# Fused RMSNorm and matmul: a new order of the first loads, of the first matmuls, of the norms, and single stores at the end

## The chip, the cores and the metric

The kernel runs on one core of a Trainium2 chip. The time is device microseconds of one execution, the median of several. A run's state is "fast" or "slow" (over 1.5% above the fastest of its kernel); verdicts use fast runs: the medians below are of all six times, the ratios of fast ones alone. Profiles come from one execution each. Their span is about 1.8 us shorter than the time of the same run.

## The reference

```python
def reference(x, gamma, weight, eps):      # x: 16 x 1024 x 512, weight: 512 x 768, float32
    rms = np.sqrt(np.mean(x ** 2, axis=-1, keepdims=True) + eps)
    x_norm = x / rms * gamma
    return np.matmul(x_norm, weight).astype(np.float32)
```

That is 16384 rows, in 128 tiles of 128 rows. 33.6 MB of x and 1.6 MB of weights come in and 50.3 MB go out.

## The kernel before

GpSimd casts x to bfloat16, TensorE transposes it (pairs of bfloat16 as one 32-bit word, so that a tile takes two transposes, called "words" below), VectorE copies the transpose out of PSUM, TensorE multiplies by the weights (gamma folded in) in four k steps, each one matmul of 512 columns and one of 256. ScalarE squares and sums rows, takes the root, VectorE the reciprocal. The result is scaled by it while it is evicted (copied out of PSUM), even tiles by ScalarE, odd ones by VectorE. Large loads and stores all go through one queue, that of the sync engine. Parts that the change and the argument touch (cuts marked; NT is the 128 tiles, NP the 64 pairs of them, K the 4 k steps; the lists say how many tiles one load of x or one store takes):

```python
    XG, OG = 16, 8
    AHEAD = 20
    ...
    opening = [1, 2, 1, 2, 2]
    last = NT // OG - 1
    x_first, x_size = stretches(XG, {0: opening + [4, 4], 1: [4, 4, 8]})
    o_first, o_size = stretches(OG, {0: opening, 1: [4, 4], last - 1: [4, 4], last: [2, 2, 2, 1, 1]})
    ...
    xin = ctx.enter_context(tc.tile_pool(name="xin", bufs=2))      # two groups of 16 tiles of x
    ...
        load_until(3)                                  # x tiles 0, then 1 and 2
        w_f32 = singles.tile([P, K, O], F32)
        for h in range(2):                             # the two weight halves
            nc.sync.dma_start(out=w_f32[:, 2 * h:2 * h + 2, :].rearrange("p c o -> p (c o)"), in_=wv[:, h, :])
        load_until(2 * XG)
    ...
        for k in (0, 1):
            for i in range(3):
                matmuls(i, acc[i], [k])
        root(0, 3, ssq)
        weights(2, nc.vector)
        weights(3, nc.scalar)
        cast(3, nc.gpsimd)
        matmuls(0, acc[0], [2, 3])
        finish_tile(0, acc[0], nc.scalar)
        transpose_tile(3)
        norms(3, 1)
        matmuls(1, acc[1], [2, 3])
        finish_tile(1, acc[1], nc.vector)
    ...
        for j in range(2, NP):                         # pairs of tiles
            load_until(2 * j + AHEAD)                  # from group 2 on: 16 tiles in one load
            if j + 3 < NP:
                cast(2 * j + 6, nc.gpsimd, 2)
            if j + 1 < NP:
                norms(2 * j + 2, 2)
            ...
            for i, engine in ((2 * j, nc.scalar), (2 * j + 1, nc.vector)):
                a = accumulator()
                matmuls(i, a, range(K), feed)          # feed: transposes of pair j + 2 in between
                finish_tile(i, a, engine)              # evict, and store when a stretch is full
```

Of the kernel before, what the change touches and what calls it, by code (L numbers as in the profile page):

```python
# [12 lines left out]
F32 = mybir.dt.float32  # L13
# [5 lines left out]
def kernel(  # L19
# [8 lines left out]
    nc = tc.nc  # L28
    P = 128

    x = x.flatten_outer_dims()
    out = out.flatten_outer_dims()
    N, D = x.shape
    _, O = out.shape
    K = D // P
    NT = N // P
    NP = NT // 2
    XG, OG = 16, 8
    AHEAD = 20
    WIDE = 512  # L40



# [2 lines left out]
    def stretches(group, parts):  # L46
        first, size, i = {}, {}, 0
        for g in range(NT // group):
            for n in parts.get(g, [group]):
                for t in range(i, i + n):  # L50
                    first[t], size[t] = i, n
                i += n
        return first, size

    opening = [1, 2, 1, 2, 2]
    last = NT // OG - 1
    x_first, x_size = stretches(XG, {0: opening + [4, 4], 1: [4, 4, 8]})
    o_first, o_size = stretches(OG, {0: opening, 1: [4, 4], last - 1: [4, 4], last: [2, 2, 2, 1, 1]})

    def rows(ap, i, n):  # L60
        if i < XG:
# [3 lines left out]
    singles = ctx.enter_context(tc.tile_pool(name="singles", bufs=1))  # L65
# [11 lines left out]
    def held(tiles, group, i, n=1):  # L77
        return tiles[i // group][:, i % group:i % group + n, :]

    def load(i):  # L80
        if i // XG not in x_tiles:
            x_tiles[i // XG] = xin.tile([P, XG, D], F32, name="xt")
        nc.sync.dma_start(out=held(x_tiles, XG, i, x_size[i]), in_=rows(x, i, x_size[i]))  # L83
# [3 lines left out]
    def load_until(i):  # L87
        while starts and starts[0] < i:
            load(starts.pop(0))

    def cast(i, engine, n=1):
        if i // 2 not in xb_tiles:
            xb_tiles[i // 2] = xbp.tile([P, 2, D], BF16, name="xb")
        engine.tensor_copy(out=xb_tiles[i // 2][:, i % 2:i % 2 + n, :], in_=held(x_tiles, XG, i, n))  # L94

    def square(i, ssq):
        jk = junk.tile([P, D], BF16, name="jk")
        nc.scalar.activation(out=jk, in_=held(x_tiles, XG, i)[:, 0, :], func=AF.Square, accum_out=ssq)  # L98

    def root(i, n, ssq):  # L100
        rms = stats.tile([P, 4], F32, name="rms")
        nc.scalar.activation(out=rms[:, :n], in_=ssq[:, :n], func=AF.Sqrt, scale=1.0 / D, bias=eps_sb)  # L102
        rstd = stats.tile([P, 4], F32, name="rstd")
        nc.vector.reciprocal(out=rstd[:, :n], in_=rms[:, :n])  # L104
        for t in range(n):
            rstd_of[i + t] = rstd[:, t:t + 1]

    def norms(i, n):
        ssq = stats.tile([P, 4], F32, name="ssq")
        for t in range(n):  # L110
            square(i + t, ssq[:, t:t + 1])
        root(i, n, ssq)
# [3 lines left out]
    def transpose_word(j, t, h):  # L116
        if j not in tp_tiles:
            tp_tiles[j] = tpsum.tile([P, 2, 2, P], F32, name="tp")
        words = xb_tiles[j].rearrange("p a d -> p (a d)").bitcast(F32)
        lo = t * (D // 2) + h * P  # L120
        nc.tensor.transpose(out=tp_tiles[j][:, t, h, :], in_=words[:, lo:lo + P], identity=ident_f)  # L121
# [9 lines left out]
    def transpose_tile(i):  # L131
        for h in range(2):
            transpose_word(i // 2, i % 2, h)
        evac(i // 2, i % 2, 1)
# [7 lines left out]
    def accumulator():  # L142
        return opsum.tile([P, 2, WIDE], F32, name="ops").rearrange("p a b -> p (a b)")

# [15 lines left out]
    def matmuls(i, acc, ks, feed=None):  # L160
        for k in ks:
            matmul(i, k, acc, 0, WIDE)
            if feed:
                feed()
            matmul(i, k, acc, WIDE, O)

    def finish_tile(i, acc, engine):
        scale(engine, out_tile(i), acc[:, :O], rstd_of[i])
        store(i)
# [14 lines left out]
        return feed  # L184

    with tc.manual_schedule():
        g_row = singles.tile([2, P, 2], F32)
        nc.scalar.dma_start(out=g_row, in_=gamma.rearrange("(h w c) -> h w c", w=P, c=2))

        wv = weight.rearrange("(h w c) o -> w h (c o)", w=P, c=2)  # L190
        touched = singles.tile([P, 2, 1], F32)
        nc.scalar.dma_start(out=touched, in_=wv[:, :, 0:1])
        nc.scalar.preload_act_table(AF.Sqrt)  # L193
        load_until(3)
        w_f32 = singles.tile([P, K, O], F32)
        for h in range(2):
            nc.sync.dma_start(out=w_f32[:, 2 * h:2 * h + 2, :].rearrange("p c o -> p (c o)"), in_=wv[:, h, :])
        load_until(2 * XG)


        warm = singles.tile([P, WIDE], BF16)
        nc.vector.memset(warm, 0.0)  # L202
        eps_sb = singles.tile([P, 1], F32)
        nc.vector.memset(eps_sb, float(eps))  # L204
        ident_f = singles.tile([P, P], F32)
        make_identity(nc, ident_f)
        spare = accumulator()

        def warm_up(n):
            for _ in range(n):  # L210
                nc.tensor.matmul(out=spare[:, :WIDE], lhsT=warm[:, :P], rhs=warm, start=True, stop=True)  # L211

        w_bf = singles.tile([P, K, O], BF16)

        def weights(k, engine, lo=0, hi=O):
            scale(engine, w_bf[:, k, lo:hi], w_f32[:, k, lo:hi], g_sb[:, k % 2, k // 2:k // 2 + 1])


        ssq = stats.tile([P, 4], F32, name="ssq")
        warm_up(6)  # L220
        cast(0, nc.vector)
        square(0, ssq[:, 0:1])
        gp = tpsum.tile([P, 2, 2], F32, name="tp")
        for c in range(2):
            nc.tensor.transpose(out=gp[:, c, :], in_=g_row[:, :, c], identity=ident_f[:2, :2])  # L225
        g_sb = singles.tile([P, 2, 2], F32)
        nc.vector.tensor_copy(out=g_sb, in_=gp)  # L227
        transpose_tile(0)
        warm_up(3)
        cast(1, nc.vector)  # L230
        cast(2, nc.gpsimd)
        square(1, ssq[:, 1:2])
        square(2, ssq[:, 2:3])
        transpose_tile(1)
        transpose_tile(2)
        warm_up(2)

        acc = [accumulator() for _ in range(4)]
        weights(0, nc.vector, 0, WIDE)
        weights(0, nc.vector, WIDE, O)  # L240
        weights(1, nc.scalar)
        for k in (0, 1):
            for i in range(3):
                matmuls(i, acc[i], [k])
        root(0, 3, ssq)
        weights(2, nc.vector)
        weights(3, nc.scalar)
        cast(3, nc.gpsimd)
        matmuls(0, acc[0], [2, 3])
        finish_tile(0, acc[0], nc.scalar)  # L250
        transpose_tile(3)
        norms(3, 1)
        matmuls(1, acc[1], [2, 3])
        finish_tile(1, acc[1], nc.vector)
        cast(4, nc.gpsimd)
        cast(5, nc.gpsimd)
        matmuls(2, acc[2], [2, 3])
        finish_tile(2, acc[2], nc.scalar)
        matmuls(3, acc[3], [0, 1, 2, 3], feeder([2], [0, 2, 2, 0], alone=True))
        finish_tile(3, acc[3], nc.vector)  # L260
        cast(6, nc.gpsimd, 2)
        cast(8, nc.gpsimd, 2)
        norms(4, 2)


        one, two, both = [1, 1, 0, 1, 1, 0, 0, 0], [1, 0, 1, 0, 1, 0, 1, 0], [1, 1, 1, 1, 1, 1, 1, 1]
        for j in range(2, NP):
            load_until(2 * j + AHEAD)
            if j + 3 < NP:
                cast(2 * j + 6, nc.gpsimd, 2)  # L270
            if j + 1 < NP:
                norms(2 * j + 2, 2)
            if j == NP - 1:
                break
            if j < 4:
                feed = feeder([j + 1], one)
            elif j == 4:
                feed = feeder([5, 6], both)
            elif j + 2 < NP:
                feed = feeder([j + 2], two)  # L280
            else:
                feed = None
            for i, engine in ((2 * j, nc.scalar), (2 * j + 1, nc.vector)):
                a = accumulator()
                matmuls(i, a, range(K), feed)
                finish_tile(i, a, engine)


        for i in (NT - 2, NT - 1):
            for lo, hi, engine in ((0, WIDE, nc.scalar), (WIDE, O, nc.vector)):  # L290
                a = accumulator()
                for k in range(K):
                    matmul(i, k, a, lo, hi)
                scale(engine, out_tile(i)[:, lo:hi], a[:, lo:hi], rstd_of[i])
            store(i)
# [35 lines left out]
```

## Time and profile before

| | before |
|---|---|
| time, median of the first 3 runs | 210.76 us |
| span of the profile | 208.6 us |
| first real matmul, last matmul's end | 8.67 us, 203.08 us |
| bytes moved by the sync queue | 85.46 MB |

A page's first section gives busy time by engine; the slices divide the span in 40, a digit is a share in tenths; a line by stretches gives busy time of PE, PEld, DVE, ACT, POOL, then granted clock, DMA share, GB/s. The chain is the work that ended last, followed back. From the page, the sync queue's line (packets, MB, share of what 16 DMA engines have in the span) and the chain's shares:

```profile
q1 hardware_dynamic: 6336, 85.46, 97.0%
q8 instruction: 10, 0.16, 0.3%
...
PE 91%; DMA 3%; DVE 1%; ACT 1%; issue 1%; SPq 0%; DVEq 0%
```

And by stretches, 40 to 60 us (busy time of PE, PEld, DVE, ACT, POOL, then granted clock, DMA share, GB/s):

```profile
40.00:60.00 20.00, 19.89 (x131) 14.06 (x133) 11.38 (x21) 15.66 (x40) 6.79 (x7) 1.00 1.01 428
```

The chain is TensorE's for 91% of the span. But 97.0% of 208.6 us are 202.3 us in which an average DMA engine moved this queue's packets; with the other queues (0.5%) it is 203.4 us. The chain and this share describe two paths of almost the same length, and a chain shows only one of them. (The share is rough to a per cent or two: in the full stretch above it reads 1.01.)

### The profile page before, as it was taken

Reading aid. Unit: us, or ns where it says so; the run is one execution under the profiler, and the core shown is the slowest. Engines: PE = TensorE matmul, PEld = TensorE weight load, DVE = VectorE, ACT = ScalarE, POOL = GpSimd, SP = SyncE. Lnnn points to the kernel's source line nnn. Section 1 sums busy time; section 2 is a strip of 40 time slices with the busy share of each in tenths; the row PEclk is TensorE's granted clock in tenths of the full one; section 3 lists DMA queues with packets and bytes.
Section 4 is the critical chain, followed back from the end, with each engine's and each line's share of the span. In section 5 each row is a group of like instructions: output and inputs, shape, how many; then the busy total and the mean of one; then the engine's idle time right before and its main releaser. Section 6 shows DMA issues by size and latency. Waiting matters only on the chain.

```text
span 208.6 us, 3553 instructions
## 1 busy us (share of the span) xinstructions
PE 199.0 (95%) x1268; PEld 137.7 (66%) x1293; DVE 111.6 (54%) x204; ACT 158.2 (76%) x388; POOL 65.8 (32%) x71
## 2 busy tenths in 40 slices
PE   7799999999999999999999999999999999999990
PEld 3366777666766776677667666766776667667650
DVE  2555654654564465456546545654664565456450
ACT  4589787787778778777877877787787778778850
POOL 1058532303631343215323063311533054230000
PEclk9999999999999999999999999999999999999999
DMA  6999999999999999999999999999999999899885
GB/s 216 399 431 415 424 398 433 478 408 394 438 448 421 410 438 434 440 412 424 448 437 432 396 438 438 434 412 432 438 427 456 405 424 437 353 443 386 361 349 225
DMA packets 6630, 85.69 MB, mean 411 GB/s; under 512 B 978, under 2 KB 980, under 8 KB 3156
## 3 DMA queue, kind: packets, MB, share of 16 engines
q1 hardware_dynamic: 6336, 85.46, 97.0%
q8 instruction: 10, 0.16, 0.3%
q10 hardware_dynamic: 276, 0.00, 0.1%
q14 instruction: 8, 0.07, 0.1%
HBM read 35.13 MB, written 50.33 MB: 410 GB/s over the span
## 4 chain that ended last, share of the span: by engine, by line
PE 91%; DMA 3%; DVE 1%; ACT 1%; issue 1%; SPq 0%; DVEq 0%
PE ops L156 78%; PE tp L121 13%; DMA w_f<-in_weight_dram 3%; DVE ot L140 1%; ACT ot L138 0%; SPq L83 0%; ACT jk L98 0%; DVE w_bf L140 0%; DVE xT L128 0%; ACT rms L102 0%; DVE rstd L104 0%; DVEq L140 0%
## 5 line engine op out<-in xcount | busy, mean ns | idle before, releaser
L156 PE MATMUL ops<-w_bf,xT 128*128 128x512 bf16 (+1 forms) x999 | 192.5, 324 | 2.8 <-DVE w_bf L140 1.4
L156 PEld LDWEIGHTS <-xT 128*128 128x128 bf16 x1024 | 100.2, 98 | 57.8 <-issue 1.9
L94 POOL CAST xb<-xt 128x1024 bf16<-128x1024 f32 (+1 forms) x65 | 65.1, 1016 | 120.0 <-PE tp L121 62.2
L128 DVE COPY xT<-tp 128x1024 bf16<-128x1024 bf16 (+1 forms) x67 | 44.5, 667 | 81.0 <-PE tp L121 81.0
L138 ACT ACTIVATE ot<-ops,rstd 128x768 f32<-128x768 f32 (+1 forms) x65 | 58.1, 895 | 37.6 <-PE ops L156 36.8
L98 ACT ACTIVATE jk<-xt 128x512 bf16<-128x512 f32 x128 | 78.7, 619 | 1.1 <-DMA xt<-in_x_dram 1.1
L121 PE MATMUL tp<-ident_f,xb 128*128 128x128 f32 x256 | 69.2, 275 | 0.1
L140 DVE TENSOR_SCALAR ot<-ops,rstd 128x768 f32<-128x768 f32 (+1 forms) x65 | 64.5, 992 | 2.9 <-PE ops L156 2.8
L121 PEld LDWEIGHTS tp<-ident_f,xb 128*128 128x128 f32 x256 | 36.1, 142 | 3.8 <-issue 0.7
L98 ACT ACTIVATION_READ_ACCUMULATOR jk<-xt 128x1 f32 x128 | 24.4, 191 | 0.0
L102 ACT ACTIVATE rms<-ssq,eps_sb 128x2 f32<-128x2 f32 (+1 forms) x64 | 18.9, 296 | 2.0
L104 DVE RECIPROCAL rstd<-rms 128x2 f32<-128x2 f32 (+1 forms) x64 | 10.0, 156 | 3.3 <-ACT rms L102 3.2
L211 PE MATMUL ops<-warm 128*128 128x512 bf16 x11 | 4.8, 585 | 1.2 <-DVE eps_sb L204 1.2
L138 ACT ACTIVATE w_bf<-w_f,g_sb 128x768 bf16<-128x768 f32 x2 | 1.9, 936 | 2.6 <-DMA w_f<-in_weight_dram 2.6
L211 PEld LDWEIGHTS <-warm 128*128 128x128 bf16 x11 | 1.4, 134 | 2.6 <-issue 1.4
L193 ACT ACT_TABLE_LOAD x1 | 1.3, 1283 | 1.8 <-issue 1.8
L94 DVE CAST xb<-xt 128x512 bf16<-128x512 f32 x2 | 1.0, 491 | 2.4 <-DMA xt<-in_x_dram 2.4
L140 DVE TENSOR_SCALAR w_bf<-w_f,g_sb 128x512 bf16<-128x512 f32 (+2 forms) x3 | 1.4, 484 | 1.2 <-DMA w_f<-in_weight_dram 1.2
L225 PEld LDWEIGHTS tp<-ident_f,g_row 2*128 2x128 f32 x2 | 0.3, 201 | 0.8 <-issue 0.8
L202 DVE MEMSET warm<- 128x256 uint32 x1 | 0.3, 272 | 0.9 <-PEq L312 0.9
L225 PE MATMUL tp<-ident_f,g_row 2*128 2x2 f32 x2 | 0.4, 264 | 0.0
L227 DVE COPY g_sb<-tp 128x4 f32<-128x4 f32 x1 | 0.2, 161 | 0.4 <-PE tp L225 0.4
(7 smaller groups left out, 1.0 us busy)
## 6 DMA issues: line engine op xcount, KB each, us to landing
out_dram<-ot SPq DMA_DIRECT2D x12, 3072.0 KB, 15.1
xt<-in_x_dram SPq DMA_DIRECT2D x6, 4096.0 KB, 19.2
out_dram<-ot SPq DMA_DIRECT2D x4, 1536.0 KB, 10.8
out_dram<-ot SPq DMA_DIRECT2D x6, 768.0 KB, 9.6
xt<-in_x_dram SPq DMA_DIRECT2D x4, 1024.0 KB, 13.9
xt<-in_x_dram SPq DMA_DIRECT2D x1, 2048.0 KB, 18.8
xt<-in_x_dram SPq DMA_DIRECT2D x3, 512.0 KB, 6.2
w_f<-in_weight_dram SPq DMA_DIRECT2D x2, 768.0 KB, 7.1
```

The source lines that it names most:

```text
L94: engine.tensor_copy(out=xb_tiles[i // 2][:, i % 2:i % 2 + n, :], in_=held(x_tiles, XG, i, n))
L98: nc.scalar.activation(out=jk, in_=held(x_tiles, XG, i)[:, 0, :], func=AF.Square, accum_out=ssq)
L102: nc.scalar.activation(out=rms[:, :n], in_=ssq[:, :n], func=AF.Sqrt, scale=1.0 / D, bias=eps_sb)
L104: nc.vector.reciprocal(out=rstd[:, :n], in_=rms[:, :n])
L121: nc.tensor.transpose(out=tp_tiles[j][:, t, h, :], in_=words[:, lo:lo + P], identity=ident_f)
L128: nc.vector.tensor_copy(out=dst[:, t:t + n, :], in_=src[:, t:t + n, :])
L138: nc.scalar.mul(out=dst, in_=src, mul=r)
L140: nc.vector.tensor_single_scalar(out=dst, in_=src, scalar=r, op=mybir.AluOpType.mult)
L156: nc.tensor.matmul(out=acc[:, lo:hi], lhsT=xT_tiles[i // 2][:, i % 2, k // 2, :, k % 2], rhs=w_bf[:, k, lo:hi], start=(k == 0), stop=(k == ...
L193: nc.scalar.preload_act_table(AF.Sqrt)
L211: nc.tensor.matmul(out=spare[:, :WIDE], lhsT=warm[:, :P], rhs=warm, start=True, stop=True)
L225: nc.tensor.transpose(out=gp[:, c, :], in_=g_row[:, :, c], identity=ident_f[:2, :2])
```

## The change

Its intent: start the matmuls as soon as half the weights and two tiles of x are there, take TensorE's early waits for VectorE away, and shorten the tail.

```diff
-    opening = [1, 2, 1, 2, 2]
+    opening = [1, 1, 1, 1, 2, 2]
-    o_first, o_size = stretches(OG, {..., last: [2, 2, 2, 1, 1]})
+    o_first, o_size = stretches(OG, {..., last: [2, 2, 1, 1, 1, 1]})
 ... (the "touch", a small early transfer of one column of the weights, is issued
      before gamma, not after it)
+        load_until(2)
+        load_weights(0)
         load_until(3)
-        for h in range(2): ... both weight halves
+        load_weights(1)
 ... (warm-up matmuls, on zeros before the real work, moved, two more; casts and squares
      of tiles 1 and 2 moved; the scale of k 2 now ahead of the root of tiles 0 to 2)
-        for k in (0, 1):
-            for i in range(3):
-                matmuls(i, acc[i], [k])
+        matmuls(0, acc[0], [0, 1])
+        transpose_tile(2)
+        matmuls(1, acc[1], [0, 1])
+        matmuls(2, acc[2], [0, 1])
 ...
+        matmuls(1, acc[1], [2, 3])
         transpose_tile(3)
+        finish_tile(1, acc[1], nc.vector)
         norms(3, 1)
-        matmuls(1, acc[1], [2, 3])
-        finish_tile(1, acc[1], nc.vector)
 ... (in the loop)
-            if j + 1 < NP:
-                norms(2 * j + 2, 2)
 ... (after the iteration's two evictions; SHIFT = 8)
+            if j <= SHIFT:
+                norms(2 * j + 2, 2)
+            if SHIFT <= j < NP - 2:
+                norms(2 * j + 4, 2)
```

More of the change, by code (lines that the diff above doesn't have):

```diff
@@ L40 @@
     WIDE = 512
+    SHIFT = 8
     def stretches(group, parts):
@@ L53, in stretches @@
         return first, size
-    opening = [1, 2, 1, 2, 2]
+    opening = [1, 1, 1, 1, 2, 2]
     last = NT // OG - 1
     x_first, x_size = stretches(XG, {0: opening + [4, 4], 1: [4, 4, 8]})
-    o_first, o_size = stretches(OG, {0: opening, 1: [4, 4], last - 1: [4, 4], last: [2, 2, 2, 1, 1]})
+    o_first, o_size = stretches(OG, {0: opening, 1: [4, 4], last - 1: [4, 4], last: [2, 2, 1, 1, 1, 1]})
     def rows(ap, i, n):
@@ L186 @@
     with tc.manual_schedule():
-        g_row = singles.tile([2, P, 2], F32)
-        nc.scalar.dma_start(out=g_row, in_=gamma.rearrange("(h w c) -> h w c", w=P, c=2))
         wv = weight.rearrange("(h w c) o -> w h (c o)", w=P, c=2)
@@ L192, with load_weights @@
         nc.scalar.dma_start(out=touched, in_=wv[:, :, 0:1])
+        g_row = singles.tile([2, P, 2], F32)
+        nc.scalar.dma_start(out=g_row, in_=gamma.rearrange("(h w c) -> h w c", w=P, c=2))
         nc.scalar.preload_act_table(AF.Sqrt)
+        w_f32 = singles.tile([P, K, O], F32)
+        def load_weights(h):
+            nc.sync.dma_start(out=w_f32[:, 2 * h:2 * h + 2, :].rearrange("p c o -> p (c o)"), in_=wv[:, h, :])
+        load_until(2)
+        load_weights(0)
         load_until(3)
-        w_f32 = singles.tile([P, K, O], F32)
-        for h in range(2):
-            nc.sync.dma_start(out=w_f32[:, 2 * h:2 * h + 2, :].rearrange("p c o -> p (c o)"), in_=wv[:, h, :])
+        load_weights(1)
         load_until(2 * XG)
@@ L227 @@
         nc.vector.tensor_copy(out=g_sb, in_=gp)
+        cast(1, nc.vector)
+        square(1, ssq[:, 1:2])
         transpose_tile(0)
-        warm_up(3)
-        cast(1, nc.vector)
-        cast(2, nc.gpsimd)
-        square(1, ssq[:, 1:2])
-        square(2, ssq[:, 2:3])
+        warm_up(2)
         transpose_tile(1)
-        transpose_tile(2)
-        warm_up(2)
+        warm_up(5)
         acc = [accumulator() for _ in range(4)]
@@ L241 @@
         weights(1, nc.scalar)
-        for k in (0, 1):
-            for i in range(3):
-                matmuls(i, acc[i], [k])
+        cast(2, nc.gpsimd)
+        square(2, ssq[:, 2:3])
+        matmuls(0, acc[0], [0, 1])
+        transpose_tile(2)
+        matmuls(1, acc[1], [0, 1])
+        matmuls(2, acc[2], [0, 1])
+        weights(2, nc.vector)
         root(0, 3, ssq)
-        weights(2, nc.vector)
         weights(3, nc.scalar)
@@ L266 @@
         one, two, both = [1, 1, 0, 1, 1, 0, 0, 0], [1, 0, 1, 0, 1, 0, 1, 0], [1, 1, 1, 1, 1, 1, 1, 1]
-        for j in range(2, NP):
+        for j in range(2, NP - 1):
             load_until(2 * j + AHEAD)
@@ L270 @@
                 cast(2 * j + 6, nc.gpsimd, 2)
-            if j + 1 < NP:
-                norms(2 * j + 2, 2)
-            if j == NP - 1:
-                break
             if j < 4:
```

## The prediction

> **What bounds the kernel now.** I read the page first (shares, slices), then the chain of work that ended last, then the waits and timelines of the first 20 us, the timeline of GpSimd's casts, and last the DMA by stretches at the end.
>
> ```profile
> span 208.6 us, 3553 instructions
> PE 199.0 (95%) x1268; PEld 137.7 (66%) x1293; DVE 111.6 (54%) x204; ACT 158.2 (76%) x388; POOL 65.8 (32%) x71
> ...
> DMA  6999999999999999999999999999999999899885
> ```
>
> TensorE is busy in 95% of the span, and the DMA engines are full too in all slices but the first and the last few. From the chain and the timelines around the start of the matmuls (start us, us, what; in the timeline also the idle time before and its releaser):
>
> ```profile
> 1.64 6.39 DMA w_f<-in_weight_dram
> ...
> 8.67 2.82 PE ops L156 x16
> 11.52 0.90 ACT ot L138
> ...
> 13.47 0.93 DVE ot L140
> ...
> 14.88 0.39 PE ops L156
> ...
> 17.00 1.48 PE ops L156 x8
> ```
>
> ```profile
> 9.93 0.62 DVE L140 TENSOR_SCALAR w_bf<-w_f,g_sb 128x768 bf16<-128x768 f32 x1 [0.48 <-DMA w_f<-in_weight_dram]
> ...
> 13.39 0.17 DVE L104 RECIPROCAL rstd<-rms 128x1 f32<-128x1 f32 x1 [1.20 <-ACT rms L102]
> 13.47 1.02 DVE L140 TENSOR_SCALAR ot<-ops,rstd 128x768 f32<-128x768 f32 x1
> ...
> 14.40 0.75 DVE L128 COPY xT<-tp 128x512 bf16<-128x512 bf16 x2
> ...
> 17.28 0.17 DVE L104 RECIPROCAL rstd<-rms 128x2 f32<-128x2 f32 x1 [1.13 <-ACT rms L102]
> ```
>
> The first weight half lands at 8.03, is scaled, and real matmuls begin at 8.67. The second half is used from 9.93. The chain leaves TensorE twice. VectorE stood 1.20 us at the reciprocal of tile 3's norm, so the eviction of tile 1 and then the copy of tile 4's transpose came late. The same pattern, smaller, ends with the copy at 17.36. From 17.00 on the chain is TensorE alone, to the last matmul at 203.08.
>
> How much idle time is that? In the chain four matmul instructions (two k steps of one tile) take 0.65 us, so a k step is 0.325; a transposed word is 0.108. From 8.67 to 14.88 are 6.21 us. The work in it is tiles 0 to 3 (16 x 0.325 = 5.20) and six transposed words (0.65), 5.85: idle 0.36. The eight instructions from 17.00 take 1.48 where 1.30 is their work: 0.18. After that a pair of tiles costs 8 x 0.325 + 4 x 0.108 = 3.03, and the casts come 3.03 to 3.04 apart: no idle time left to remove. So TensorE can gain only before 18.5 us, and the tail after 203.08 is the other place.
>
> Loads matter too. GpSimd's casts (one per pair of tiles) and the tail, by stretches (the last two numbers are the DMA share and GB/s):
>
> ```profile
> 50.38 4.00 POOL L94 CAST xb<-xt 128x1024 bf16<-128x1024 f32 x4 [9.68 <-DMA xt<-in_x_dram]
> ...
> 71.33 3.01 POOL L94 CAST xb<-xt 128x1024 bf16<-128x1024 f32 x3 [6.34 <-DMA xt<-in_x_dram]
> ```
>
> ```profile
> 202.00:203.00 1.00, 1.00 (x7) 0.49 (x5) 0.29 (x1) 0.39 (x2) 0.00 (x0) 1.00 0.73 301
> 203.00:204.00 1.00, 0.07 (x1) 0.00 (x0) 0.48 (x1) 0.35 (x1) 0.00 (x0) 1.00 1.02 412
> ```
>
> The group of tiles 32 to 47 lands at 50.38; its first cast ends at 51.4 and TensorE transposes that pair at 52.16. That is 0.7 us of slack, the smallest of all groups: at 71.33 and later it is 3 to 4 us.
>
> **What the Trainium skill says.** "PSUM — Partial Sum Buffer", section "Engine vs sequencer instructions": the queues of ScalarE, VectorE and GpSimd are strict FIFO. The trace agrees: the copy at 14.40, whose input was there, stood behind the reciprocal and the eviction. "TensorE: Matmul & The Clock Gate", section "Back-to-back issue gap": N/2.4 + 2.5 ns warm, 215.8 ns for 512 columns and 109.2 for 256, 0.325 together; the chain's 0.65 for two k steps agrees. "DMA: Bandwidth & Descriptors", section "Where 436 GB/s comes from": the fabric ends at about 435 GB/s; the stretches of 20 us from 20 to 180 show 424 to 438, so loads can't come faster, only in another order. Same page, section "Queues, rings and completion order": each DMA engine takes its ring's descriptors in order. The trace fits: the load of tiles 32 to 47, issued at 29.53, landed about 20.8 us later, behind what was queued.
>
> **The change part by part.**
> Load order. The first weight half now follows 512 KB of x instead of 768. Between the two weight halves the trace shows 1.8 us for 768 KB, so 256 KB are 0.6 us: it lands near 7.4 instead of 8.03, and matmuls start near 8.0 instead of 8.67. But the bytes ahead of the second half are the same, so it is still used from 9.93.
> Order of matmuls. TensorE goes tile by tile: tile 0, k 0 and 1 (0.65, with some 0.15 more, as k 1 needs ScalarE's 0.94 us scale of the second k slice, ready near 8.4), two words of tile 2 (0.22, formerly done before the start), tiles 1 and 2 (1.30). That ends near 10.3. Then k 2 needs 9.93 + 0.62 of VectorE's scaling and 0.05 of signal: 10.6. Before, TensorE reached the same step at 8.67 + 6 x 0.325 = 10.62. So the earlier start is worth nothing: it becomes 0.3 us of waiting for the second half.
> Norms after evictions. Tile 3's norm now comes after tile 1's eviction, and its transposes after tile 1's matmuls (which also takes away 0.05 of waiting for the cast at 10.62). From 10.6: ten k steps and six words, 3.90, tile 4 starts at 14.5 instead of 14.88. VectorE copies tile 3 near 12.2, evicts tile 1 until 13.6, and copies tile 4 by 14.2: in time. Gain 0.36. In the loop the norms of pairs 3 to 8 come after the evictions of the iteration, so the reciprocal at 17.28 no longer stands ahead of a copy: another 0.18. Together 0.54.
> Norms "two pairs ahead". From iteration 8 on, norms of pair j+2 at the end of iteration j stand, on ScalarE and VectorE, in the very place where norms of pair j+1 at the start of iteration j stood. So nothing changes there but the iteration of 8, where two norms follow one another: 2 x 1.7 us of ScalarE, which makes the next eviction about 1.2 us late. There are three accumulators, so TensorE is not held.
> The load of tiles 32 to 47 waits for the square of tile 15, which now runs after the eviction of tile 12: its issue comes about 1.5 us later than 29.53. At that time about 14.7 MB are issued and 11.3 moved (sum of the stretches), so some 3.4 MB or 8 us lie in the queue ahead of it: the landing stays. TensorE asks for it 0.54 us earlier, of 0.7 us slack: no stall.
> Warm-up matmuls are moved and two more are made; they end before the weights. Zero.
> Last stores. Four single tiles instead of a pair and two singles. The pair's store was issued at 201.60 and most engines idled from 201.95 to 202.45, then ran without a break to about 206.4 (one engine to 207.2). With tile 124 issued near 200.2 that hole of 0.5 is filled. Gain 0.5; one more issue of 0.33 us on the sync queue is hidden.
> Sum: 0.54 + 0.5 = 1.05, and about 0.1 for shorter last waits: 1.15. Span 207.45, time 210.76 - 1.15 = 209.6.
>
> **The rivals.**
> A: the early start is kept. If the second half too were usable earlier by 0.3, TensorE would be 0.85 ahead at 18 us, over the 0.7 us slack at 52: the stall caps it, and the time would be about 209.4. For it: the touch of the weights is now the first small transfer. Against: the bytes ahead are the same.
> B: the loads take it back. If the later issue of tiles 32 to 47 delays their landing by 1 us or more, TensorE stalls by 0.8 or more at 52 and the head's gain is gone: 210.3, and with 1.5 us 210.8. For it: the landing took about 1.7 us more than its queued bytes explain, and slack is thin. Against: the 8 us of queue.
> C: the tail is kept from gaining because one engine ends last, 0.7 us after the others, whatever the order of the stores: 210.1. For it: that straggler. Against: it idled in the hole too, as far as its packets can be put in line.
> D: the DMA bounds everything, nothing moves: 210.7. Against: engines idle in the last 10 us (share 0.73 at 202), so the end is not set by bytes alone.
>
> **Range and chances.** Main path 209.6; A 209.4, C 210.1, B 210.3 to 210.8. Runs scatter by 0.3 us. 8 times in 10: 209.0 to 210.4. Faster by over 2% needs under 206.5, four times the sum of all that I can find; the chance is 0.02. Slower by over 2% needs a stall of over 4 us; 0.01. Within 2%: 0.97.
>
> **What would show it.** Step one is right if the chain's first weight DMA ends near 7.4 and the first matmul starts near 8.0, yet TensorE waits for VectorE's weight scale and k 2 of tile 0 starts near 10.6. Step two: no wait of VectorE's reciprocal ahead of a copy in 12 to 18 us; tile 4 starts near 14.5; the casts' rhythm is 0.5 to 0.6 us earlier. Step three: the cast of tiles 32 to 33 starts near 50.4 as before, with no gap of TensorE near 52. Step four: the last matmul ends near 202.5, no DMA hole near 201.5, and the time from it to the end is 5.0 instead of 5.5. A later cast at 50.4, with a gap on TensorE, would make B right; a stall of the evictions or copies in iterations 2 to 9 would make my reading of the norms wrong.

## The result and the profile after

The changed kernel took 210.95 us (median of 6 runs, 210.34 to 213.99, one of them slow), the kernel before 210.81 us (6 runs). The ratio is 1.0006, 95% interval 0.9987 to 1.0026: no difference. A ratio here is the mean time of one kernel's fast runs over that of the other's of the same rounds, so not quite the ratio of the medians. Predicted were 209.6 us and a range of 209.0 to 210.4; the time lies above it.

The page after:

```profile
span 209.8 us, 3564 instructions
...
q1 hardware_dynamic: 6768, 85.46, 96.7%
...
PE 81%; DMA 14%; POOL 1%; issue 1%; SPq 1%; DVE 1%; POOLq 0%
PE ops L157 69%; PE tp L122 12%; DMA xt<-in_x_dram 10%; DMA w_f<-in_weight_dram 4%; POOL xb L95 1%; SPq L84 1%; DVE w_bf L141 0%; DVE ot L141 0%; SPq L198 0%; POOLq L95 0%
```

A load of x has come into the chain with 10% of the span. The profiled run was the longest of the fast ones (211.54 us), which is why its span is 209.8. The chain in order of time (start us, us, what), from the opening:

```profile
2.58 7.71 DMA w_f<-in_weight_dram
...
10.31 0.63 DVE w_bf L141
...
10.99 1.46 PE ops L157 x8
...
17.05 1.30 PE ops L157 x8
```

The same view from 46 us on, where it goes back to the load of tiles 32 to 47:

```profile
31.42 20.91 DMA xt<-in_x_dram
...
52.48 1.05 POOL xb L95
...
53.57 0.33 PE tp L122
```

The stretch from 40 to 60 us, to be held against the one of before:

```profile
40.00:60.00 20.00, 18.51 (x122) 12.86 (x122) 10.43 (x20) 15.42 (x40) 6.20 (x7) 1.00 1.00 420
```

And from the timeline of VectorE, the reciprocal of tile 3's norm, now with no idle time before it:

```profile
13.97 0.15 DVE L105 RECIPROCAL rstd<-rms 128x1 f32<-128x1 f32 x1
```

The opening did part of what was wanted. The reciprocal of tile 3 no longer waits, and the eight instructions from 17.05 take 1.30 us where before they took 1.48. But the second weight half is used from 10.31, not 9.93, and TensorE starts its k 2 at 10.99. Taken together TensorE is only 0.13 us ahead afterwards: casts that wait for it come at 30.41, 33.46 and 36.49 us, before at 30.54, 33.59 and 36.62. Then the load of tiles 32 to 47 lands at 52.33, 2 us later than before, and TensorE is busy for 18.51 us of the stretch instead of 19.89. After that everything is 1.5 us late, and the last matmul ends at 204.55 instead of 203.08. From there to the end it takes 5.25 us instead of 5.52.

The packet records of the two traces say more of that load. 90% of its packets had ended at 47.59 us before and at 47.90 after, but the last one at 49.89 before and 52.04 after. Its last packets end about 1.2 us apart, which is what one packet of this load takes, so I take it that one DMA engine, behind the others, finishes alone; the records do not name engines. The trace also has 16 completion records (semaphore increments) for this load, which fit that: the last but one came at 49.72 before and 50.57 after, the last at 50.23 and 52.33. The load's first packet started at 37.46 before and 37.41 after, so its turn in the queue was not later.

### The profile page after: what moved, and what is told of

It reads as the page before. It is cut to its first block, busy times and chain, and to the rows that moved or that the text cites. A ratio compares the mean times of both kernels' runs of the same rounds, so it can differ in the third digit from the quotient of the medians.

```text
span 209.8 us, 3564 instructions
## 1 busy us (share of the span) xinstructions
PE 199.9 (95%) x1270; PEld 138.0 (66%) x1295; DVE 111.9 (53%) x204; ACT 158.2 (75%) x388; POOL 65.7 (31%) x71
## 3 DMA queue, kind: packets, MB, share of 16 engines
q1 hardware_dynamic: 6768, 85.46, 96.7%
## 4 chain that ended last, share of the span: by engine, by line
PE 81%; DMA 14%; POOL 1%; issue 1%; SPq 1%; DVE 1%; POOLq 0%
PE ops L157 69%; PE tp L122 12%; DMA xt<-in_x_dram 10%; DMA w_f<-in_weight_dram 4%; POOL xb L95 1%; SPq L84 1%; DVE w_bf L141 0%; DVE ot L141 0%; SPq L198 0%; POOLq L95 0%
## 5 line engine op out<-in xcount | busy, mean ns | idle before, releaser
L217 PE MATMUL ops<-warm 128*128 128x512 bf16 x13 | 5.5, 580 | 1.2 <-DVE eps_sb L210 1.2
## 6 DMA issues: line engine op xcount, KB each, us to landing
out_dram<-ot SPq DMA_DIRECT2D x4, 768.0 KB, 10.5
```

What stands on the lines that cost most here:

```text
L217: nc.tensor.matmul(out=spare[:, :WIDE], lhsT=warm[:, :P], rhs=warm, start=True, stop=True)
```

## The experiments

There were 18 runs (16 kernels, two of them run twice), each for 5 rounds beside the kernel before, so each has 6 times. Theory T: what takes an early start of TensorE back is the load of tiles 32 to 47. Theory F, later: two such "absorbers" stand in a row, that load and, behind it, the full DMA engines. Rivals: a chance profile, the late issue of that load, loss in the changed order itself.

**1. The changed kernel again.** No edit.

> The changed kernel a second time, to see what of its profile repeats. Theory T (the load of tiles 32 to 47 lands behind its slowest DMA engine, and lands later than TensorE wants it): TensorE again stands between 50 and 54 us, 0.5 to 2 us, and the span is 0.13 us of earlier start plus that stall away from before; ratio to before 1.00 within 0.3%. Rival N (the first profile was a chance slow one): no stall near 52 us, and the time is 0.2 to 0.5% under before.

211.17 us, ratio to before 1.0019 (0.9996 to 1.0043). Its profile repeats the first one: the second weight half is used from 10.38, the load of tiles 32 to 47 lands for a cast at 52.44, TensorE is busy 18.61 us of the 20 from 40 to 60. The chance profile (N) is out. The runs reach from 210.48 to 212.19; those of before on that chip from 210.48 to 211.26.

**2. Changed kernel, that load in two halves; 3. kernel before, same edit.**

```diff
-    x_first, x_size = stretches(XG, {0: opening + [4, 4], 1: [4, 4, 8]})
+    x_first, x_size = stretches(XG, {0: opening + [4, 4], 1: [4, 4, 8], 2: [8, 8]})
-            load_until(2 * j + AHEAD)
+            load_until(2 * j + AHEAD + (8 if j == 7 else 0))
```

> The changed kernel with the load of tiles 32 to 47 cut in two loads of 8 tiles, issued one after the other at the same place. Theory T: the first half lands some 4 to 5 us before the whole did, near 47 to 48 us, the stall of TensorE near 52 us is gone, the time falls by 0.4 to 0.8%, to 209.3 to 210.1 us. Rival N: nothing changes, within 0.2%. Rival Q (the queue is slower as a whole after the change, not its landing): tiles 40 to 47 or a later group become late, TensorE stalls later, less than 0.3% is won.

> The kernel before with the same cut of the load of tiles 32 to 47. Theory T: its landing was early enough by 0.7 us, so the time stays within 0.15% of before. If it gains more than 0.3%, the kernel before loses time there too in executions that the first profile did not show.

The stall near 52 is gone in both: 19.84 us busy from 40 to 60, and the first half's cast is at 47.02 and 45.94 us. The times: 210.76 us (1.0019, interval 0.9982 to 1.0056) and 210.74 us (1.0013, 0.9979 to 1.0047). So the stall is removed and the time does not fall; T's number failed. The profile of the kernel before with the edit shows why. From its page:

```profile
span 209.1 us, 3554 instructions
...
DMA  6999999999999999999999999999999999998983
```

And the last piece of its chain, the eviction after the last matmul:

```profile
202.02 0.48 DVE ot L140
```

In that execution the weights came early (scaled from 7.1 and 8.8 us), nothing held TensorE, and it was done at 202.00, 1.08 us before the kernel before. Yet the span is 0.5 us longer: the end now comes 7.1 us after the last matmul, and the packet records show the last store's packets at 90% by 206.93 and complete at 207.76 us. The DMA engines were behind. (The profile of the changed kernel with the edit, 211.6 us, had its second weight half at 12.0 us and is not used for the end.)

**4. Changed kernel, norms of the loop back at the start of the iteration.**

```diff
+            norms(2 * j + 2, 2)
             if j < 4:
 ...
-            if j <= SHIFT:
-                norms(2 * j + 2, 2)
-            if SHIFT <= j < NP - 2:
-                norms(2 * j + 4, 2)
```

> The changed kernel with the norms of the loop back at the start of the iteration, all else kept. Rival B of the prediction (the load of tiles 32 to 47 is late because it is issued late, as it waits for the square of tile 15): the load is issued near 29.4 us instead of 31.4 and lands near 50.4 again, the stall near 52 us is gone, about 0.5% faster than the changed kernel. Theory T (the landing is set by bytes ahead and the slowest engine): issued near 29.4, landed at 51.5 or later, the stall stays, time within 0.2% of the changed kernel; and a 0.2 us gap of TensorE near 18 us comes back.

210.97 us (1.0027, 0.9997 to 1.0057). The load is issued at 30.02 us instead of 31.42 and the cast that it releases is at 52.23 instead of 52.48 (timeline of GpSimd):

```profile
52.23 4.99 POOL L95 CAST xb<-xt 128x1024 bf16<-128x1024 f32 x5 [11.04 <-PE tp L122]
```

(The view puts the wait down to TensorE, whose transposes had long freed the buffer; the load's last completion record is at 52.09, against 52.33.) 1.4 us of earlier issue gave 0.24 us of earlier landing, so rival B's mechanism (late because issued late) is not the cause. Some stall stays (19.38 us busy), smaller as TensorE itself comes later.

**5 and 6. Half of the middle stores left out, results wrong.**

```diff
+            if n == OG:
+                n = OG // 2
             nc.sync.dma_start(out=rows(out, first, n), in_=held(o_tiles, OG, first, n))
```

> Wrong on purpose: the kernel before, storing only half of the tiles of the twelve middle groups (18.9 MB of 85.5 fewer), so that the DMA queue has room and TensorE's path alone sets the time. Theory F (in the kernel before, TensorE's path and the fullest DMA engine end within about 1 us of each other): TensorE's path is untouched, last matmul near 203 us, span 208.0 to 208.8, so no more than 0.4% under before. Rival (before waits for the DMA in the middle too): 1% or more faster.

> Wrong on purpose: the changed kernel with the same half of the stores. Theory F: without a full queue the load of tiles 32 to 47 is in time, no stall near 52 us, and the changed kernel is now faster than half_before by 0.3 to 0.6% (0.5 to 1.2 us: the part of the sum in the prediction that the late second weight half leaves, plus the tail). Rival (the change gains TensorE nothing, its own order stalls): the two are within 0.15%.

210.26 us (0.9983, 0.9964 to 1.0001) and 211.18 us (1.0026, 0.9993 to 1.0060). The second expectation failed. Both still waited near 52 us (casts at 51.01 and 51.78; 19.31 and 19.52 us busy from 40 to 60), because the stores that are left out come after that load. So these two did not separate the effects, and I ran them again with the load cut in two (14 to 17).

**7 and 8. 13.6 us less of TensorE, same bytes, results wrong.**

```diff
-            matmul(i, k, acc, WIDE, O)
+            if k != 2:
+                matmul(i, k, acc, WIDE, O)
```

> Wrong on purpose: the kernel before without the 256-column matmul of k 2 in all but the last two tiles, 126 x 0.108 = 13.6 us less of TensorE, the same bytes. Theory F: the DMA sets a floor only 0 to 1.5 us under the time of before: span 207 to 209, under 1% faster. Rival (TensorE is the bound, as the prediction had it): 5 to 6% faster, span near 196.

> Wrong on purpose: the changed kernel without the same matmuls. Theory F: the same floor or up to 0.4 us later, as the weights land 0.4 us later in its opening: 0 to 0.2% slower than less_before. Rival (the changed order of loads and stores helps the queue itself): faster than less_before by 0.2% or more.

210.76 us (1.0002, 0.9984 to 1.0021) and 210.28 us (0.9986, 0.9967 to 1.0005). This is the central result: with 126 matmul instructions fewer TensorE is done at 198.5 us instead of 203.08, and the time of the kernel before does not move. The page of less_before:

```profile
span 209.0 us, 3326 instructions
...
PE   7698999998999999999999979998999979999900
...
DMA  6999999999999999999999999999999999999991
...
q1 hardware_dynamic: 6336, 85.46, 96.7%
...
PE 50%; DMA 35%; ACT 5%; POOL 2%; DVE 1%; issue 1%; SPq 1%; POOLq 0%; DVEq 0%
```

The last piece of its chain:

```profile
198.53 0.48 DVE ot L140
```

And of less_after:

```profile
span 208.5 us, 3337 instructions
...
DMA  6999999999999999999999999999999999999991
...
q1 hardware_dynamic: 6768, 85.46, 97.1%
```

The DMA digits are 9 to the last slice but one, and the chain has gone over to the loads, by 35% in the first. Note that PE still shows 90% busy in the first of them (188.9 us instead of 199.0): the busy share alone would not have told. A slower clock does not hide the saving: it was granted at half from 8.8 to 12.2 us and in full from there to the last matmul, which can cost 1.7 of the 13.6 us at most (an estimate). The queue's share of the span is what it was in the kernel before: 96.7% of 209.0 are 202.1 us, 97.1% of 208.5 are 202.5. The DMA floor of this program is that of the whole kernel, 210.3 to 210.8 us. Between the two, 0.2%, no difference is certain (expected was 0 to 0.2% slower, it came out faster); the change is not shown to raise or lower the floor.

**9 and 10. Why do the weights land later? Parts of the opening undone in the changed kernel.**

```diff
 gamma_first: gamma is issued before the touch of the weights, as in before
 together:
-        load_until(2)
-        load_weights(0)
         load_until(3)
+        load_weights(0)
         load_weights(1)
```

> The changed kernel with the two small transfers on the scalar queue in their old order (gamma, then the touch of the weights). So far the second weight half was used from 8.7 to 10.0 us in four profiles with the opening of before, and from 10.3 to 10.5 (once 12.0) in six with the changed opening. Theory O (the order of the small transfers makes the weights late): used from 8.7 to 10.0 again, and faster than the changed kernel by 0.2% or more. Theory I (the third x tile between the halves makes it late) and theory P (three single x tiles make it late): it stays at 10.2 or later, time within 0.15% of the changed kernel.

> The changed kernel with x tiles 0, 1, 2 (single) and then both weight halves, so that the third tile is not between the halves. Theory I: the second half is used from 8.7 to 10.0, the first near 8.0, time 0 to 0.4% under the changed kernel. Theories O and P: the second half stays at 10.2 or later, time within 0.15% of the changed kernel.

211.18 us (1.0011, 0.9983 to 1.0040), second half from 10.7; and 211.14 us (1.0010, 0.9978 to 1.0042), second half from 10.3. So these profiles, one of each, do not show the order of the small transfers or the third tile between the halves to be the cause alone.

**11. Singles.** The kernel before with `opening = [1, 1, 1, 1, 2, 2]` only.

> The kernel before with only x tiles 1 and 2 (and their stores) as single tiles, load order as before. With the opening of before, the second weight half was used from 8.7 to 10.0 us in six profiles; with the changed opening from 10.2 to 10.8 in seven (once 12.0), whatever the order of the small transfers or of the third tile. Theory P (the single tiles make the weights late): 10.2 or later. If it is used from 8.7 to 10.0, the single tiles alone are not the cause. Time within 0.2% of before either way, by theory F.

211.54 us (1.0025, 0.9991 to 1.0059). The second half was used from 9.5 us, within what openings of before give. So single tiles alone are not shown to be the cause either, nor is the half's later issue (one more load stands ahead of it on the sync queue, 2.58 instead of 2.1 us), which this kernel shares. That the changed opening's weights come later is seen in every profile of it. In the nine profiles with the opening loads of before, the first half was used from 6.9 to 8.2 us (median 7.15) and the second from 8.7 to 10.0 (8.95); in the eight with the changed opening from 7.8 to 9.6 (8.0) and from 10.3 to 12.0 (10.5). The first profile of before was among the late ones, so the 0.4 us seen beside it understate the loss. Even the first half, with 256 KB less ahead of it, came later, not earlier. Why, stays open.

**12 and 13. Two parts of the change alone in the kernel before.**

```diff
 tail_only:
-    last: [2, 2, 2, 1, 1]
+    last: [2, 2, 1, 1, 1, 1]
 norms_only: the norms of the loop after the evictions, and tile 3's norm after
 the eviction of tile 1, as in the changed kernel; opening and stores as before
```

> The kernel before with only the last four tiles stored singly. The prediction's step four: the DMA hole of 0.5 us near 202 is filled and the time falls by 0.5 us, 0.24%. Theory F (the fullest DMA engine sets a floor near 208.5 us of span whatever TensorE does): less than 0.1%, as that engine has no hole to fill; the last store still lands 3.5 us or more after it is issued.

> The kernel before with only the norms moved (in the loop and of tile 3), opening and stores as before. The prediction's step two: TensorE's gaps near 14.6 and 18 us go, tile 4 and all after it come 0.4 to 0.55 us earlier for the same landing of the weights; the time falls by 0.2% if TensorE is the bound. Theory F: gained by TensorE at 20 us, but the time stays within 0.1% of before, the gain being lost at 52 us or in a longer tail.

Tail only: 210.54 us, 0.9987 (0.9961 to 1.0012). That interval holds both zero and the predicted 0.24%; it is undecided. Norms only: 211.18 us, 1.0006 (0.9981 to 1.0031). Its profile shows the first absorber at work (by stretches):

```profile
40.00:60.00 20.00, 18.37 (x121) 12.66 (x120) 10.33 (x19) 14.67 (x37) 6.02 (x6) 1.00 1.00 418
```

The last piece of its chain:

```profile
203.45 0.48 DVE ot L140
```

The weights came early in it (8.9) and the gaps were gone. From the first matmul to the loop's first transpose it took 6.32 us (7.62 to 13.94) against 6.60 before (8.67 to 15.27), and from there to the transpose that follows the eight matmul instructions of that stretch 3.04 instead of 3.21 (before 15.27 to 18.48). That is 0.45 us of the 0.54 predicted. TensorE was 1.5 us ahead of before at that point, lost all of it and more waiting near 52, and ended at 203.43 against 203.08.

**14 to 17. Both absorbers taken away: half the middle stores and the split load, in both kernels, twice.** The edits are those of 5 and 2, results wrong.

> Wrong on purpose: the kernel before with half of the middle stores and the load of tiles 32 to 47 cut in two, so that neither the queue nor that load can hold TensorE. Theory F (two absorbers in a row: the wait at 52 us, then the DMA floor): only here an earlier start comes through: no stall near 52, last matmul at 201.5 to 202.9 depending on when the weights land (8.8 or 9.9), span 206.8 to 208.2, 0.4 to 0.9% under before.

> Wrong on purpose: the same in the changed kernel. The prediction's sum holds only if it is 0.5% faster than half_split_b. Theory H (the changed opening makes the second weight half 0.4 to 1.5 us later, which takes back the 0.54 us won by the norms): last matmul 202.5 to 203, the same as half_split_b or up to 0.3% slower, no stall near 52.

> half_split_b again, on the same chip as half_split_a2, to see whether the difference repeats and to have a profile. Time 209 to 210.2, last matmul 202 to 203.

> half_split_a again: its five fast runs were 0.7% under half_split_b, but its profile fell in the slow one. If the change shortens TensorE's path as the prediction summed (1.15 us, 0.55%), it is again 0.4 to 0.8% faster than half_split_b2, and a fast profile shows no stall of TensorE after 11 us, the last matmul at 202.0 or earlier and the end 5 us after it. If theory H held after all, it is within 0.2% of half_split_b2.

First pair: kernel before 209.84 us (0.9937 of the whole kernel before), changed 208.25 us (0.9869). Fast runs alone: means 209.68 and 208.22, 0.7% in favour of the change. Second pair: 209.48 and 210.08 us, means of fast runs 209.57 and 209.53, no difference. The single times explain that. The changed kernel has seven of its twelve runs at 208.09 to 208.37 and the rest at 209.8 to 212.2; the kernel before has all twelve at 209.08 to 210.24. The best of each are 1.0 us apart; the means of all fast runs, 208.88 and 209.63, are 0.75 us apart, 0.4%. So with room in the queue the change's better runs gain about what the prediction summed, and its other runs nothing; theory H does not hold in the first pair and does in the second. Both profiles of the changed kernel fell on long runs. The chain of the later one shows what such a run is made of:

```profile
2.59 9.06 DMA w_f<-in_weight_dram
...
11.67 0.63 DVE w_bf L141
```

The second half was used from 11.67 us; in half_split_b2 it was 9.83. From there to the last matmul's end it took 192.6 us, against 193.1 in half_split_b2 and in half_split_b; from the last matmul to the end 4.87, against 5.27 and 5.25. So the norms and the tail did gain 0.9 us here, and weights that came 1.8 us later took it back. That the short runs are those whose weights came early is likely; no profile fell on one, so it is not shown.

**18. The version that the experiments point to.** Opening of before, norms moved, load of tiles 32 to 47 cut in two, single stores at the end.

> The best candidate that the experiments point to: the opening of before, the norms moved, the load of tiles 32 to 47 cut in two, the last four tiles stored singly. Rival (the gains add up once the stall at 52 is gone): 1 us or more faster, 209.7. Theory F (DMA engines busy 203.3 us each with the same bytes, from 1.8 us on): TensorE is done 1 us or more earlier than in before, near 201.5, and the time stays within 0.2% of before, 210.3 to 210.7; the tail after the last matmul grows to 6.5 us or more.

210.59 us, 0.9982 (0.9961 to 1.0003). From its page:

```profile
span 208.8 us, 3555 instructions
...
DMA  6999999999999999999999999999999999998992
...
q1 hardware_dynamic: 6624, 85.46, 96.9%
```

The last piece of its chain:

```profile
201.56 0.48 DVE ot L140
```

TensorE is done at 201.54, 1.54 us earlier than in the kernel before, and the end comes 7.3 us later. All of the gain on TensorE lies in front of the DMA floor. It is not shown to beat before, and no kernel with these bytes in these packets did.

## Why the prediction was wrong, point by point

**The bound.** The prediction held that TensorE's chain sets the end and that "the end is not set by bytes alone", because DMA engines idle in the last 10 us. The premise was right and the conclusion was not: these idle moments were about all the DMA had. An estimate from the page of before: 203.4 us of packets for an average engine, nothing moved before about 1.7 us, and the end comes some 1.4 us after the last packet (207.2 of 208.6), in sum 206.5 of 208.6 us. The 1.15 us that the prediction summed would have had to come out of 2.1 us of idle time, evenly on all 16 engines, with one of them ending 0.7 us late. (It is rough: packets overlap a little, by the shares of 1.00 to 1.02 in full stretches, so the idle time is somewhat more.) That is the step that failed, rival D's dismissal. What the runs showed in its place: TensorE done 4.6 us earlier (experiment 7) or 1.1 to 1.5 us earlier (3 and 18), and the end where it was. In the changed kernel's own profile the gain was gone before that, in the next two steps; taking the wait near 52 us away (2) brought nothing back.

**No stall near 52.** The slack of 0.7 us was read from one profile. There the weights had come late and the load fairly early. In other profiles with the opening of before that load's cast came at 50.82 (tail_only), 51.01 (half_before) and 51.35 us (norms_only), and TensorE lost time there in all three. It is a meeting point: whoever comes early waits. The reason given in rival B, late issue, is not it (experiment 4), and the prediction's 8 us of queue were right: the load's first packet started at 37.41, before at 37.46. What came 2.1 us later is the last of its 16 completions, 1.76 us behind the one before it where it was 0.51 behind. Why it lags stays open. The prediction weighed the stall only with late issue, and that its number for B (210.8) was near is luck.

**The weights.** The early start was worth nothing, as forecast, but not for the reason given: with the same bytes ahead, the second half still came 0.4 us later than before in the first pair of profiles, and about 1.5 us later between the medians of all. The first was scaled from 7.87, not 7.4. This term of the sum was 0 and measured 0.37 us against TensorE in the first pair (10.99 instead of 10.62). Its cause is open.

**The gaps.** Right: 0.54 us predicted, 0.45 us measured (norms_only), 0.5 in half_split_a2.

**The norms two pairs ahead.** Not refuted: from iteration 8 on nothing was to change, and no profile shows a stall there.

**The tail.** 0.5 us predicted, 0.27 us between the last matmul and the end in the first two profiles, 0.4 in half_split_a2 where the queue has room. With all bytes moved it is undecided: 0.13% in tail_only, with an interval that includes zero.

**The sum.** On TensorE's path, set free, the change gains 0.75 us (0.4%) in the mean of two unequal pairs and 1.0 us between best runs, against 1.15 us predicted. The sum was about right for a kernel that is not this one, and whose weights do not come late.

## What to carry to other kernels

Before you sum gains along a chain, multiply the DMA queue's share of the span by the span: if that, plus the start and the last landing, comes as close to the span as here (206.5 of 208.6 us), the chain is only one of two bounds, and the gain is limited by the idle time of the DMA engines. The quickest test is a kernel with the same bytes and much less work on the engine that seems to bind. And slack read from one profile is one draw; where two streams meet, look at several executions before you count on tenths of a microsecond.

## What the Trainium skill lacked or had wrong

- "Perfetto Trace Analysis", section "Identifying the Most-Contended Engine", calls occupancy of the 16 DMA engines misleading and sends the reader to HBM utilization. Here the DMA share was not misleading: it was 97.0% of 208.6 us, and with 13.6 us less of TensorE the time stayed at 210.76 us. The profile's HBM rate, 410 GB/s over the span beside 424 to 438 in full stretches, points the same way.
- "DMA: Bandwidth & Descriptors", section "Where 436 GB/s comes from", says that for transfers between HBM and SBUF the HBM side, about 358 GB/s, binds, though it names 425 as measured. Here, with one core running, 424 to 438 GB/s were sustained in 20 us stretches from 20 to 180 us, of loads and stores together, so 358 did not bind.
- "TensorE: Matmul & The Clock Gate", section "Back-to-back issue gap", gives about 131 ns a matmul as the sustained rate at N=512 and says that the formula N/2.4 + 2.5 over-counts. Here the next matmul followed one of 512 columns after 216 ns and one of 256 after 109 ns (medians in before), in a continuous stream, as that formula has it.
- No page gives a figure for how far the 16 DMA engines drift apart within one load. The last packet of the load of tiles 32 to 47 ended 2.3 us (before) and 4.1 us (after) behind the first 90% of its packets.
- No page tells of the scatter of first loads: in nine profiles with the same opening, the second weight half was used from 8.7 to 10.0 us, in eight with the changed one from 10.3 to 12.0 us.
